# The masked relative bias of the neighbourhood heads: two products of rounded parts in place of one full-float product

## The chip, the core and the metric

The kernel runs on one core of a Trainium2 chip. The time is that of the device in microseconds (us), from the start to the end of one execution. It is measured over several runs; one further execution is recorded by the profiler, and its page and trace are read below.

## What is computed

Two layers of a diffusion backbone over 256 latent tokens (a grid of 4 rows of 64) with 256 context tokens. Each layer is feed-forward, token mixing, feed-forward. The mixing has three parts side by side: six neighbourhood heads of width 64, six heads of latent attention (MLA), and a state-space part. This case is about the neighbourhood heads' scores, in the reference:

```
s_win = einsum('brqhd,brkhd->bhrqk', qg, kg) * scale + bias      # bias: gathered from rpb by grid offset
s_win = where(in_win, s_win, NEG_INF)                            # 16 columns around the query
s_ctx = einsum('brqhd,bkhd->bhrqk', qg, kc) * scale
p = softmax(concatenate([s_win, s_ctx]))
```

Every latent query sees all 256 context keys and, of the 256 latent keys, those in its column window, with a learned bias that depends on the row and column distance. In layer 0 the context queries are computed too (over context keys, with no bias); in layer 1 only latent queries are.

## The kernel before

All activations lie transposed in SBUF. Almost all products are made by `mm3` (L287 to L293): each operand is split into a rounded part and the rest (type F32R), and three products of such parts stand for one full product. Full-float products are used in few places: transposes against the identity, scores, value products, and the product looked at here.

Weights come in units in a fixed order; `take` gives a unit, loads the one three ahead and splits the next (ScalarE copies to the rounded type, L251; VectorE or GpSimd subtracts, L252). Inside a unit the order of the work on every engine is the order in which the program writes it: each engine takes its own instructions in turn, and a waiting one holds up all that stand behind it on that engine.

`mixers` makes queries, keys and values, then calls `attention` (L1431), then multiplies by `w_out`. Just ahead of `attention` stand the last lines of the state-space gate: two copies on ScalarE (L1383) and one subtraction each on VectorE and GpSimd (both L1384). Before that, `bias` (128 x 36 x 64) has been filled by DMA with shifted rows of the bias table, its query columns running backwards; `window` (L1425, on GpSimd) adds the mask, 0 or -1e30, to six of its rows at a time, that is to one head. Heads 0 and 1 are masked before `attention`, head h + 2 while head h is scored.

`attention` opens its own pool of buffers and goes through a list of jobs: for each pair of heads, two query tiles per head ("x", latent queries), and in layer 0 one job per head for the context queries ("c"). Step i of its loop writes:

- `scores` of job i: for a neighbourhood head one product of queries and keys, 64 x 128 against 64 x 512 (L1458), then the bias product (L1463), which adds into the right half of the same sums: the constant matrix at `K_FLIP`, which turns the query columns back, times 256 columns of `bias`. Then the maximum on VectorE (L1470) and the Exp on ScalarE (L1474);
- `scale` of job i - 1: reciprocal and scaling on VectorE (L1479, L1481);
- `transposes` of job i - 3: four transposes on TensorE (L1490), emptied by VectorE or ScalarE in turn (L1493, L1495; L1498 for "c");
- at i = 4 `k_cols`: the transposes of the MLA keys (L1117, tile kn); at i = 6 the split of the next weights (`ahead`);
- `pv`, two steps after a pair is complete: value products (L1510), then a ScalarE copy and a VectorE subtraction that split the output (L1513, L1514).

Score sums have four buffers (`acc`), transposes three and sometimes a fourth.

Of the kernel before, what the change touches and what calls it, by code (L numbers as in the profile page):

```python
# [10 lines left out]
F32 = mybir.dt.float32  # L11
F32R = mybir.dt.float32r
AF = mybir.ActivationFunctionType
OP = mybir.AluOpType
# [22 lines left out]
K_ID, K_SEL, K_WIN, K_COS, K_SIN, K_DEL, K_ONE, K_FLIP, K_END = 0, 128, 130, 194, 258, 322, 338, 466, 594  # L37
# [56 lines left out]
class Net:  # L94
# [1336 lines left out]
    def attention(self, l, need, nq, nv, mq, mv, bias, ox, k_cols):  # L1431
        nc = self.nc
        V, P, S = nc.vector, nc.gpsimd, nc.scalar
        mm = nc.tensor.matmul
        with lines(self.tc, name=f"att{l}", bufs=1) as ap:
            def views(h):
                if h < 6:
                    r = slice(64 * (h % 2), 64 * (h % 2) + 64)
                    return nq[0][r, h // 2, :], nq[1][r, h // 2, :], lambda kt: nv[:, kt, 64 * h:64 * h + 64]
                return mq[0][:, h - 6, :], mq[1][:, h - 6, :], lambda kt: mv[:, kt, h - 6, :]  # L1440
# [8 lines left out]
                        jobs.append(("c", h, 0))  # L1449
            PT = {}  # L1450
            st = {}

            def scores(j):
                kind, h, t = j
                q, k, v = views(h)
                s = self.acc()
                if kind == "x":
                    mm(s, q[:, 256 + 128 * t:384 + 128 * t], k, start=True, stop=h >= 6)  # L1458
                    if h < 6:
                        if t == 0:  # L1460
                            self.window(bias, h + 2)
                        b = bias[:, 6 * h + 2 - 2 * t:6 * h + 6 - 2 * t, :].rearrange("p s k -> p (s k)")
                        mm(s[:, 256:512], self.k[:, K_FLIP:K_FLIP + 128], b, start=False, stop=True)  # L1463
                    nb, n = 1, 512
                else:
                    for i in range(2):
                        mm(s[:, 256 * i:256 * i + 256], q[:, 128 * i:128 * i + 128], k[:, 0:256], start=True, stop=True)
                    nb, n = 2, 256
                m = ap.tile([128, 2], F32, name="m", bufs=4)
                V.tensor_reduce(m[:, 0:nb], s.rearrange("p (b n) -> p b n", b=nb), axis=AX, op=OP.max, negate=True)  # L1470
                e = ap.tile([128, 512], F32, name="e", bufs=4)
                su = ap.tile([128, 2], F32, name="su", bufs=4)
                for i in range(nb):
                    S.activation(e[:, i * n:i * n + n], s[:, i * n:i * n + n], AF.Exp, bias=m[:, i:i + 1], accum_out=su[:, i:i + 1])  # L1474
                st[j] = (e, su, nb, n)
# [7 lines left out]
            def transposes(j):  # L1483
                kind, h, t = j
                e = st.pop(j)[0]
                if (kind, h) not in PT:
                    PT[kind, h] = ap.tile([128, 4 if kind == "x" else 2, 256], F32, name=f"PT{kind}", bufs=3)
                p = self.tp()
                for i in range(4):
                    nc.tensor.transpose(p[:, 128 * i:128 * i + 128], e[:, 128 * i:128 * i + 128], self.ident)  # L1490
                if kind == "x":
                    if t:
                        V.tensor_copy(PT[kind, h][:, :, 128 * t:128 * t + 128], p.rearrange("p (k q) -> p k q", k=4))  # L1493
                    else:
                        S.activation(PT[kind, h][:, :, 128 * t:128 * t + 128], p.rearrange("p (k q) -> p k q", k=4), AF.Copy)  # L1495
                    done = t == 1
                else:
                    S.activation(PT[kind, h].rearrange("p k (t q) -> p t k q", t=2), p.rearrange("p (t k q) -> p t k q", t=2, k=2), AF.Copy)  # L1498
                    done = True
                if done and h % 2:  # L1500
                    pend.append((kind, h))
# [17 lines left out]
            for i in range(len(jobs) + LAG):  # L1519
                if i < len(jobs):  # L1520
                    scores(jobs[i])
                if 0 < i <= len(jobs):
                    scale(jobs[i - 1])
                if i >= LAG:
                    transposes(jobs[i - LAG])
                if i == 4:
                    k_cols()
                if i == 6:
                    self.ahead()
                for a in old.pop(0):  # L1530
                    pv(*a)
                old.append(pend[:])
                pend.clear()
# [48 lines left out]
```

## Time and profile before

| | |
|---|---|
| time, median of 3 runs (lowest to highest) | 1960.9 us (1960.06 to 1961.4) |
| the profiled execution | 1962.65 us, of which the span from first to last instruction is 1960.7 us |
| TensorE (PE) busy | 1907.6 us, 97% of the span |
| VectorE (DVE), ScalarE (ACT), GpSimd (POOL) busy | 46%, 35%, 29% |
| mean granted clock of TensorE | 0.988 |

The clock is that which the chip granted to TensorE as a share of full speed, 2.4 GHz; the other level seen is 0.50, 1.2 GHz. Matmul records are pipelined: they overlap, and their ends are modelled, so the distance between the starts of neighbours is the better price. "PEld" is the loading of weights into the array, which can run beside a product. A full-float product leaves two records, a product of rounded parts one.

### The profile page before, as it was taken

What the parts mean: (1) busy time and instruction counts of PE and PEld (TensorE: products, weight loads), DVE (VectorE), ACT (ScalarE), POOL (GpSimd) and SP (SyncE); (2) the same over time, 40 slices, a digit from 0 to 9 for tenths busy, and PEclk for the clock granted to TensorE, in tenths of its full rate; (3) what the DMA queues carried; (4) which work ended last, traced back from release to release, by engine and by line L of the source; (5) the groups of instructions that cost most, each with busy time, mean ns of one, the idle gap of its engine ahead of it and who ended that gap; (6) DMA issues with size and microseconds to landing.
All of it is one profiled execution on the core that took longest, in us unless ns stands there. A gap on an engine that the chain in (4) does not pass through costs nothing.

```text
span 1960.7 us, 28001 instructions
## 1 busy us (share of the span) xinstructions
PE 1907.6 (97%) x11345; PEld 1557.8 (79%) x11345; DVE 907.3 (46%) x1596; ACT 678.8 (35%) x1128; POOL 574.3 (29%) x661
## 2 busy tenths in 40 slices
PE   7999999999999999999999999999999988999999
PEld 4777777788896587788888877777788878579999
DVE  6453233246457835232333554423433745655555
ACT  4421222224355634222212342122223435445343
POOL 2137461124535032100101314746212545231000
PEclk9999999999999999999999999999999999799999
DMA  9656566534431024533232455656523453036563
GB/s 309 178 166 200 174 205 212 165 97 141 132 105 51 2 86 130 173 117 96 88 105 76 139 158 167 201 160 217 178 75 113 141 166 100 22 126 215 175 194 108
DMA packets 364100, 277.75 MB, mean 142 GB/s; under 512 B 29854, under 2 KB 355812, under 8 KB 363972
## 3 DMA queue, kind: packets, MB, share of 16 engines
q1 hardware_dynamic: 361008, 268.44, 44.3%
q0 software_dynamic: 1888, 7.31, 1.0%
q8 instruction: 89, 1.46, 0.3%
q10 hardware_dynamic: 1076, 0.22, 0.1%
q14 instruction: 39, 0.32, 0.0%
HBM read 263.39 MB, written 12.55 MB: 141 GB/s over the span
## 4 chain that ended last, share of the span: by engine, by line
PE 84%; DVE 6%; POOL 4%; DMA 2%; ACT 1%; SPq 1%; issue 1%; POOLq 0%; ACTq 0%; DVEq 0%
PE acc L291 24%; PE acc L292 24%; PE acc L293 23%; PE b L467 3%; PE acc L1458 2%; PE t L1490 1%; DVE xm L562 1%; PE t L1510 1%; POOL ss L1134 1%; DVE xn L572 1%; PE acc L1463 1%; POOL sqs L523 1%; PE t L1100 1%; DMA bias<-in_na_rpb 1%; DVE xn L570 1%
## 5 line engine op out<-in xcount | busy, mean ns | idle before, releaser
L291 PE MATMUL acc<-xn,spl 128*128 128x512 f32 (+1 forms) x1664 | 598.0, 359 | 8.2 <-ACT mv L1340 5.9
L292 PE MATMUL acc<-xn,spl 128*128 128x512 f32 (+1 forms) x1664 | 590.7, 355 | 1.9 <-DVE xn L396 0.2
L293 PE MATMUL acc<-xn,spl 128*128 128x512 f32 (+1 forms) x1664 | 587.3, 353 | 0.1
L252 DVE TENSOR_TENSOR spl<-raw,spl 128x1024 fp32r<-128x1024 f32 (+2 forms) x312 | 390.2, 1287 | 276.0 <-ACT spl L251 273.8
L251 ACT ACTIVATE spl<-raw 128x1024 fp32r<-128x1024 f32 (+3 forms) x344 | 324.0, 990 | 303.9 <-PE acc L293 159.6
L291 PEld LDWEIGHTS acc<-xn,spl 128*128 128x128 f32 x1664 | 315.1, 189 | 71.7 <-issue 17.8
L292 PEld LDWEIGHTS acc<-xn,spl 128*128 128x128 f32 x1664 | 315.3, 189 | 46.7 <-DVE xn L570 4.3
L672 POOL TENSOR_TENSOR hid<-hv,hid 128x512 fp32r<-128x512 f32 (+1 forms) x88 | 101.8, 1156 | 852.2 <-ACT hid L671 852.2
L293 PEld LDWEIGHTS acc<-xn,spl 128*128 128x128 f32 x1664 | 315.3, 189 | 44.7 <-DVE spl L252 0.9
L291 PE MATMUL acc<-hid,spl 128*128 128x512 f32 (+1 forms) x740 | 265.2, 358 | 0.0
L292 PE MATMUL acc<-hid,spl 128*128 128x512 f32 (+1 forms) x740 | 262.0, 354 | 0.0
L293 PE MATMUL acc<-hid,spl 128*128 128x512 f32 (+1 forms) x740 | 261.7, 354 | 0.0
L669 DVE TENSOR_TENSOR hv<-sl,acc 128x512 f32<-128x512 f32 (+1 forms) x88 | 54.7, 621 | 365.1 <-PE acc L293 353.4
L671 ACT ACTIVATE hid<-hv 128x512 fp32r<-128x512 f32 (+1 forms) x88 | 50.9, 579 | 382.0 <-DVE hv L669 382.0
L729 DVE SCALAR_TENSOR_TENSOR h<-acc,mod,h 128x256 f32<-128x256 f32 x192 | 85.0, 479 | 210.8 <-PE acc L293 210.8
L291 PEld LDWEIGHTS acc<-hid,spl 128*128 128x128 f32 x740 | 139.8, 189 | 25.2 <-issue 6.4
L293 PEld LDWEIGHTS acc<-hid,spl 128*128 128x128 f32 x740 | 139.9, 189 | 19.7
L292 PEld LDWEIGHTS acc<-hid,spl 128*128 128x128 f32 x740 | 140.0, 189 | 18.5
L252 POOL TENSOR_TENSOR spl<-raw,spl 128x768 fp32r<-128x768 f32 (+3 forms) x32 | 65.3, 2041 | 211.4 <-ACT spl L251 199.5
L291 PE MATMUL acc<-spl,xn 128*128 128x384 f32 (+1 forms) x322 | 111.5, 346 | 0.0
L292 PE MATMUL acc<-spl,xn 128*128 128x384 f32 (+1 forms) x322 | 106.9, 332 | 0.4 <-POOL spl L252 0.3
L293 PE MATMUL acc<-spl,xn 128*128 128x384 f32 (+1 forms) x322 | 106.5, 331 | 0.0
(358 smaller groups left out, 1996.8 us busy)
## 6 DMA issues: line engine op xcount, KB each, us to landing
raw<-in_ffn_w_gu SPq DMA_DIRECT2D x176, 512.0 KB
raw<-in_w_mod SPq DMA_DIRECT2D x64, 1024.0 KB
raw<-in_ffn_w_down SPq DMA_DIRECT2D x32, 1024.0 KB
raw<-in_ffn_w_down SPq DMA_DIRECT2D x16, 768.0 KB
raw<-in_w_in SPq DMA_DIRECT2D x16, 768.0 KB
pmod<-in_w_mod SPq DMA_DIRECT2D x8, 1024.0 KB
raw<-in_w_out SPq DMA_DIRECT2D x8, 1024.0 KB
cld<-CL POOLq DMA_DIRECT2D x8, 576.0 KB, 4.8
```

Of the source, the lines that this page charges most:

```text
L251: nc.scalar.activation(s[:, 0, a:b], raw[:, a:b], AF.Copy)
L252: (nc.gpsimd if mix and b == n else nc.vector).tensor_tensor(s[:, 1, a:b], raw[:, a:b], s[:, 0, a:b].bitcast(F32), op=OP.subtract)
L291: mm(out, sl[0], sr[0], start=start, stop=False)
L292: mm(out, sl[0], sr[1], start=False, stop=False)
L293: mm(out, sl[1], sr[0], start=False, stop=stop)
L467: nc.tensor.matmul(p[32 * j:32 * j + 32, 0:256], self.cs[:, k, 6 - 2 * w:38 - 2 * w], raw[:, k, :], start=(a == 0 and w == 0), stop=(a == ...
L523: nc.gpsimd.tensor_tensor(self.sq_sum[:, c], self.sq_sum[:, c], s[:, c], op=OP.add)
L669: nc.vector.tensor_tensor(hv[:, c], sl[:, c], pu[:, c], op=OP.mult)
L671: nc.scalar.activation(hd[:, 0, c], hv[:, c], AF.Copy)
L672: nc.gpsimd.tensor_tensor(hd[:, 1, c], hv[:, c], hd[:, 0, c].bitcast(F32), op=OP.subtract)
L729: self.nc.vector.scalar_tensor_tensor(self.h[:, n, c], ps[:, c], self.mod[l][:, gate, n, s:s + 1], self.h[:, n, c], op0=OP.mult, op1=OP.add)
L1458: mm(s, q[:, 256 + 128 * t:384 + 128 * t], k, start=True, stop=h >= 6)
```

## The change

The full-float bias product is replaced by two products of rounded parts. At the start of `attention` VectorE copies the flip matrix into a tile of the rounded type. For each job of a neighbourhood head `parts` splits its 256 columns of the masked bias: ScalarE copies them to the rounded type, VectorE subtracts that from the original, which gives the second part. Both parts are multiplied by the flip matrix into the same sums. The parts of the first job are made ahead of the loop; those of each following job are written behind the bias products of the job before, ahead of that job's maximum. The parts have two buffers. The tiles for the transposed scores of the context jobs have two buffers instead of three.

```diff
             PT = {}
             st = {}
+            flip = ap.tile([128, 128], F32R, name="flip")
+            V.tensor_copy(flip, self.k[:, K_FLIP:K_FLIP + 128])
+            bp = {}
+
+            def parts(h, t):
+
+                if h < 6:
+                    b = bias[:, 6 * h + 2 - 2 * t:6 * h + 6 - 2 * t, :]
+                    bp[h, t] = ap.tile([128, 2, 4, 64], F32R, name="bp", bufs=2)
+                    S.activation(bp[h, t][:, 0], b, AF.Copy)
+                    V.tensor_tensor(bp[h, t][:, 1], b, bp[h, t][:, 0].bitcast(F32), op=OP.subtract)
+
+            parts(0, 0)
...
                     if h < 6:
                         if t == 0:
                             self.window(bias, h + 2)
-                        b = bias[:, 6 * h + 2 - 2 * t:6 * h + 6 - 2 * t, :].rearrange("p s k -> p (s k)")
-                        mm(s[:, 256:512], self.k[:, K_FLIP:K_FLIP + 128], b, start=False, stop=True)
+                        for i in range(2):
+                            mm(s[:, 256:512], flip, bp[h, t][:, i].rearrange("p s k -> p (s k)"), start=False, stop=i == 1)
+                        parts(*((h, 1) if t == 0 else (h + 1, 0)))
...
-                    PT[kind, h] = ap.tile([128, 4 if kind == "x" else 2, 256], F32, name=f"PT{kind}", bufs=3)
+                    PT[kind, h] = ap.tile([128, 4 if kind == "x" else 2, 256], F32, name=f"PT{kind}", bufs=3 if kind == "x" else 2)
```

## Rows read from the trace of the kernel before

**Rows 1.** The page: TensorE's busy time; the chain that ended last, by line.

```profile
PE 1907.6 (97%) x11345; PEld 1557.8 (79%) x11345; DVE 907.3 (46%) x1596; ACT 678.8 (35%) x1128; POOL 574.3 (29%) x661
...
PE acc L291 24%; PE acc L292 24%; PE acc L293 23%; PE b L467 3%; PE acc L1458 2%; PE t L1490 1%; DVE xm L562 1%; PE t L1510 1%; POOL ss L1134 1%; DVE xn L572 1%; PE acc L1463 1%; POOL sqs L523 1%; PE t L1100 1%; DMA bias<-in_na_rpb 1%; DVE xn L570 1%
```

**Rows 2.** By stretches: length, busy PE, PEld, DVE, ACT, POOL (instructions), clock, DMA share, GB/s.

```profile
630.00:640.00 10.00, 10.00 (x57) 5.79 (x56) 8.59 (x18) 5.60 (x16) 3.47 (x2) 1.00 0.33 106
```

**Rows 3.** Timeline, layer 0, mid-stage: start, duration, engine, line, tiles, shape, count.

```profile
626.22 0.70 PE L1463 MATMUL acc<-bias,k 128*128 128x256 f32 x2
626.75 0.60 PE L1490 MATMUL t<-k,e 128*128 128x128 f32 x4
...
628.33 0.70 PE L1463 MATMUL acc<-bias,k 128*128 128x256 f32 x2
...
631.52 1.95 PE L1510 MATMUL t<-PTx,nv 128*64 128x256 f32 x16
```

**Rows 4.** Timeline, layer 1, second feed-forward: products of rounded parts, 256 columns.

```profile
1749.82 0.28 PE L291 MATMUL acc<-xn,spl 128*128 128x256 f32 x1
1749.94 0.28 PE L292 MATMUL acc<-xn,spl 128*128 128x256 f32 x1
```

**Rows 5.** Timeline, layer 0, start of attention (in brackets: idle before, and releaser).

```profile
611.31 0.70 PE L1463 MATMUL acc<-bias,k 128*128 128x256 f32 x2
...
612.91 0.69 DVE L1384 TENSOR_TENSOR xn<-zq,xn 128x512 fp32r<-128x512 f32 x1
...
613.61 1.27 POOL L1384 TENSOR_TENSOR xn<-zq,xn 128x512 fp32r<-128x512 f32 x1 [3.50 <-ACT xn L1383]
...
614.91 1.29 DVE L1470 TENSOR_REDUCE m<-acc 128x1 f32<-128x512 f32 x2 [1.31 <-POOL xn L1384]
...
617.77 0.63 PE L1490 MATMUL t<-k,e 128*128 128x128 f32 x4 [0.72 <-DVE e L1481]
```

**Rows 6.** Timeline of TensorE at three waits; then stretches as in rows 2.

```profile
529.76 0.65 PE L1100 MATMUL t<-C,H 64*64 64x128 f32 x8 [1.30 <-POOL H L1083]
...
602.01 0.79 PE L291 MATMUL acc<-xn,spl 128*128 128x512 f32 x1 [3.41 <-ACT mv L1340]
...
1666.87 0.66 PE L1117 MATMUL t<-k,qn 128*96 128x128 f32 x2 [3.32 <-DVE mqT L1125]
...
606.00:608.00 2.00, 2.00 (x9) 1.54 (x8) 1.09 (x4) 1.78 (x3) 2.00 (x3) 0.55 0.00 0
...
1664.00:1686.60 22.60, 19.73 (x40) 8.92 (x41) 12.28 (x27) 8.25 (x20) 10.89 (x13) 0.55 0.00 1
1686.60:1700.00 13.40, 13.40 (x70) 7.54 (x67) 10.14 (x18) 7.96 (x16) 2.46 (x1) 1.00 0.02 7
```

**Rows 7.** Timeline, layer 1, start of attention, as in rows 5.

```profile
1669.89 1.22 PE L1463 MATMUL acc<-bias,k 128*128 128x256 f32 x2
...
1671.04 2.07 PE L1458 MATMUL acc<-nkT,nqT 64*128 64x512 f32 x2
...
1672.60 0.69 DVE L1470 TENSOR_REDUCE m<-acc 128x1 f32<-128x512 f32 x1 [0.77 <-POOL xn L1384]
...
1680.36 1.06 PE L1490 MATMUL t<-k,e 128*128 128x128 f32 x4
...
1685.22 1.06 PE L1117 MATMUL t<-k,kn 128*96 128x128 f32 x4
```

**Rows 8.** Timeline, layer 1, mid-stage: ScalarE and VectorE in one job.

```profile
1699.96 0.37 ACT L1513 ACTIVATE xn<-t 128x256 fp32r<-128x256 f32 x1
...
1700.37 0.42 DVE L1514 TENSOR_TENSOR xn<-t,xn 128x256 fp32r<-128x256 f32 x1
...
1700.71 0.68 DVE L1470 TENSOR_REDUCE m<-acc 128x1 f32<-128x512 f32 x1
...
1701.42 0.69 ACT L1474 ACTIVATE e<-acc,m 128x512 f32<-128x512 f32 x1 [1.09 <-DVE m L1470]
...
1702.10 0.59 ACT L1495 ACTIVATE PTx<-t 128x512 f32<-128x512 f32 x1
```

## Prediction

> **What bounds the kernel now.** I read the page first. TensorE is busy 97% of the span; the three lines of `mm3` hold 71% of the chain that ended last, the line of the bias product 1% [rows 1]. So a change to that product moves the time only by what it does to TensorE's order in `attention`, which runs once per layer. The table by stretches shows what kind of stage that is: in mid-stage TensorE has work in all of 10 us, VectorE in 8.6, ScalarE in 5.6, at the full clock [rows 2]. TensorE sets the end there, with VectorE close behind it. Next I read TensorE's own timeline in mid-stage, where the starts of neighbours give prices that the modelled ends don't. A bias product starts at 626.22, the transposes behind it at 626.75, the next job's bias product at 628.33: a job of a neighbourhood head takes 2.11 us, its bias product 0.53 [rows 3]. Last I read the start of the stage in either layer on all engines, since that is where the change puts new work ahead of the first bias product [rows 5, 7].
>
> **What is removed on TensorE.** 24 full-float bias products (6 heads, 2 query tiles, 2 layers; 48 records), each 0.53 us between starts [rows 3]. In their place come 48 products of rounded parts with the same 256 columns. The trace has that form elsewhere: in the second half of layer 1 `mm3` starts one every 0.12 us [rows 4]. I read the 0.53 as two records of about 0.213 plus 0.107 in which its first weight load stands open behind the 64-row score product, and keep the 0.107, since that neighbour stays. New price: 0.107 + 2 x 0.12 = 0.35 us, a gain of 0.187 us per job. If the second load stands open too the gain is 0.08, if none does 0.29. At half the clock the old product takes 1.15 us (1669.89 to 1671.04 [rows 7]): 0.30 and a stream of 0.85. The new pair's stream would double to about 0.43: 0.72 in all, a gain of 0.43. All 24 at full clock are worth 4.5 us, 0.23% of the time: no more is on offer there.
>
> **What is added off TensorE.** Per job a ScalarE copy of 128x256 and a VectorE subtraction of 128x256; the nearest rows of these shapes are 0.37 and 0.42 us [rows 8]. Once per layer a VectorE copy of 128x128 (I take 0.2 us, half of that subtraction, with 0.42 as the upper bound). Two buffers instead of three for the context heads' transposed scores cost nothing: their next use comes six jobs after, the product that frees them five jobs after. Summed, VectorE gets 10 us more and ScalarE 9 us more over both layers, under the cover of TensorE; but that cover is not loose. The copy for the next job stands in ScalarE's order behind the Exp of the job before, and the subtraction in VectorE's order ahead of the next maximum. This closes a circle that was not there: maximum to Exp 0.71, Exp to the next ScalarE instruction 0.68, copy to subtraction 0.41, subtraction to maximum 0.34 [rows 8], 2.14 us in all, and about 2.7 in every second job, where ScalarE also empties a transpose (0.59). Their mean of 2.42 meets TensorE's new pace, 2.11 - 0.187 plus a quarter of a value product of 1.95 us [rows 3], which is 2.41. In mid-stage it is a tie, and the transposes, which trail three jobs behind, give some 2.9 us of slack (two jobs of 2.11 less about 1.3 from maximum to scaled scores), so I let TensorE keep its gain there.
>
> **The wait at the start, layer 0.** Today the first bias product needs nothing from this stage and starts at 611.31 [rows 5]. VectorE, though, writes nothing in the stage's pool before 614.91: its first maximum waits there for GpSimd's subtraction of 613.61, and in layer 1 the first maximum (1672.60) is released by the same line [rows 5, 7]. In the new kernel the first writes into that pool are the flip copy and the first rounded part, and the bias product stands behind them: flip at 614.9, ScalarE copy 614.9 to 615.3, subtraction to 615.75, bias product at 615.8. If only VectorE's queue holds them back (its subtraction of 612.91 ends at 613.60), it is 614.35. So TensorE, in order, stands idle 3.0 to 4.5 us after its first score product, with all later scores and transposes behind it. I take 4.5. At full clock the first transposes would come at 621.1, because the maxima go at the circle's pace (616.35, 618.55, 620.75) and the fourth bias product needs the part subtracted just ahead of 620.75. That is 3.3 us after 617.77 [rows 5].
>
> **The clock.** Such a wait doesn't come alone. TensorE's wait of 3.41 us ahead of 602.01 and that of 3.32 us ahead of 1666.87 were each followed by work at half the clock, 1.2 GHz; one of 1.30 us (529.76) was not [rows 6]. 4.5 us is longer than either, so I expect the low clock from about 615 us. How long? Layer 1 goes through this stage's start at the low clock already: the mean from 1664 to 1686.6 is 0.55, though the engine works without a gap from 1667.9 on, and it is 1.00 only behind that [rows 6], once the transposes of the MLA keys have begun at 1685.22 [rows 7]. So I price layer 0 by layer 1's rows: from the first bias product to the first transposes 10.47 us (1669.89 to 1680.36), less 4 x 0.43 for the new form, 8.8. The transposes start at 615.8 + 8.8 = 624.6, 6.8 us late. Two sets of transposes (0.4 us more each) and one context score (1.05 more) at the low clock make it 8.7 late at the transposes of the MLA keys. I set their own low-clock stretch (+0.6) against TensorE's short waits for VectorE there now (-0.6). The remaining 8 jobs give back 8 x 0.187 = 1.5. Layer 0: +7.2 us.
> The Trainium skill (TensorE: Matmul & The Clock Gate, section "What's actually happening") says that the throttled state is the default and that activity releases it. Layer 1's rows, 17 us of recorded work at half the clock, agree only if these full-float products don't count as such activity; by the plain rule the low clock would end soon after the wait, which is the first rival below.
>
> **Layer 1.** The clock is low there before and after. The first bias product moves from 1669.89 to 1673.5 (the pool is free at 1672.6, then 0.4 for the copy and 0.45 for the subtraction): +3.6. Five jobs at the low clock give back 5 x 0.43 = 2.1, the transposes of the MLA keys slip behind the place where the clock rose (+0.6), and seven jobs at full clock give back 1.3. Layer 1: +0.8 us.
>
> **Sum.** The profiled execution took 1962.65 us (span 1960.7 and 1.95 around it), 1.75 above the median of the runs. 1962.65 + 7.2 + 0.8 = 1970.65; on the scale of the median 1968.9, so **1969 us**, 0.4% slower. A measurement of this kernel can tell about 0.2%, 3.9 us, from no change.
>
> **Rivals.**
> The clock returns with the work. After the wait ahead of 602.01 dense rounded products brought it back in 606 to 608 us (mean 0.55, so at 607.8 [rows 6]), 5.8 us after the wait. From 615.8 that is 621.6; the first transposes would start at 623.1, 5.3 us late. Less 1.5, plus layer 1's 0.8: 1965.5 us. Against it: layer 1's stretch.
> The clock doesn't fall. Then layer 0 is 3.3 less 1.5, with up to 1 us of VectorE's backlog on top: about +2.3, in sum 1964 us. Against it: both longer waits [rows 6].
> Not slower: the rounded pairs are dense work like that of 602 us, and lift the clock within the first two jobs of layer 1, so that two low-clock scores, two sets of transposes and one more score run at full rate. That takes some 4.7 us off layer 1 and 3 off layer 0's loss: 1961 us. It decides if the clock rises before about 1677. Against it: they are 0.43 us of a low-clock job of 3.7.
> Worse: the circle, not TensorE, sets the pace, and the low clock outlasts the transposes of the MLA keys in layer 0. No gain in mid-stage (+2.8), and four more jobs at 3.7 instead of 2.1 us (+6): 1977 us.
>
> **How the numbers follow.** Forecast 0.52 (its own range 1965 to 1973), clock returns 0.15, doesn't fall 0.13, lifted 0.08, worse 0.12. The range 1961 to 1977 reaches the ends of these. Faster by over 0.2% (below 1957) needs the full 4.5 us with no wait, or a clock lifted earlier still: 0.04. Within 0.2% (up to 1964.8): the lifted case, most of "doesn't fall" and a little of "returns", 0.22. Slower: 0.74.
>
> **What the new profile would show.** The wait: TensorE idle 3 to 4.5 us ahead of the first bias product of layer 0, released by VectorE's subtraction. The price: starts 0.35 us apart from bias pair to transposes in mid-stage. The clock: 0.50 from 615 to about 630 us. The circle: VectorE's subtraction waiting for ScalarE's copy in nearly every job. I am wrong in the main term if the clock stays at 1.00 there, and in the small ones if a job in mid-stage doesn't fall from 2.11 to about 1.93 us.

## The result and the profile after

The changed kernel takes 1984.0 us (median of 4 runs, 1979.8 to 1986.1), the kernel before beside it 1961.2 (4 runs, 1960.1 to 1962.3): a ratio of 1.0114, 95% interval 1.0096 to 1.0132. It is slower by 22.9 us. The forecast was 1969 with a range to 1977: the sign was right, the size was missed by 15 us, and the time lies outside the range.

The profiled execution of the changed kernel took 1979.84 us. Its page shows TensorE busy for nearly as long as before (1907.6 us, [rows 1]) in a longer span, and VectorE and ScalarE busier by 15.7 and 7.9 us:

```profile
PE 1910.4 (97%) x11345; PEld 1558.7 (79%) x11345; DVE 923.0 (47%) x1622; ACT 686.7 (35%) x1152; POOL 574.4 (29%) x661
```

All of the loss lies in the two runs of `attention`. Measured on TensorE from the first score product to the first product of the output projection, layer 0 went from 83.1 to 97.2 us and layer 1 from 65.3 to 72.5, together +21.2. Outside of it the two profiles differ only ahead of the first attention: that of before shows 6.8 us at the low clock from 539.5 us on and 6.8 from 601.0 on, that of after none and 3.4 us there, and its first attention starts 3.5 us earlier. So the two profiled executions differ by only 17.2 us. I cut each attention where the score products of the last job of a neighbourhood head start (in layer 0 that is the context job of head 5). The second halves, the MLA heads, are unchanged to 0.2 us. The whole 21 us is in the first halves: 42.6 to 56.6 us and 35.2 to 42.6 us.

**The start.** The timeline of after, layer 0; columns as in [rows 5], on whose place it stands:

```profile
606.76 1.12 PE L1471 MATMUL acc<-nkT,nqT 64*128 64x512 f32 x2
...
610.61 1.26 POOL L1384 TENSOR_TENSOR xn<-zq,xn 128x512 fp32r<-128x512 f32 x1 [2.47 <-ACT xn L1383]
...
611.90 0.87 DVE L1453 CAST flip<-k 128x128 fp32r<-128x128 f32 x1 [1.30 <-POOL xn L1384]
...
611.90 0.72 ACT L1461 ACTIVATE bp<-bias 128x256 fp32r<-128x256 f32 x2 [1.37 <-POOL xn L1384]
...
612.70 2.10 DVE L1462 TENSOR_TENSOR bp<-bias,bp 128x256 fp32r<-128x256 f32 x2
...
612.92 0.55 PE L1476 MATMUL acc<-bp,flip 128*128 128x256 f32 x1 [5.04 <-DVE flip L1453]
613.85 0.58 PE L1476 MATMUL acc<-bp,flip 128*128 128x256 f32 x1 [0.38 <-DVE bp L1462]
614.36 2.07 PE L1471 MATMUL acc<-nkT,nqT 64*128 64x512 f32 x2
...
622.41 1.05 PE L1504 MATMUL t<-k,e 128*128 128x128 f32 x4
```

Both first writes into the stage's pool (the flip copy, the first rounded part) start at 611.90, released by GpSimd's subtraction of L1384, as the prediction had it. TensorE waits 5.04 and 0.38 us, and then works at 1.2 GHz: a 64-row score product that took 1.12 us at 606.76 takes 2.07 at 614.36. By the trace's record the clock fell at 610.7, inside the wait, and came back at 627.7.

**The split.** The second place was not in the prediction. `ahead` issues the split of the next weights at job 6; on ScalarE and VectorE it stands between the parts of job 7 and those of job 8. This is what the timeline shows there in layer 0:

```profile
635.19 1.99 ACT L251 ACTIVATE spl<-raw 128x1024 fp32r<-128x1024 f32 x2
...
636.26 1.23 DVE L252 TENSOR_TENSOR spl<-raw,spl 128x1024 fp32r<-128x1024 f32 x1 [0.47 <-ACT spl L251]
637.08 0.40 ACT L1461 ACTIVATE bp<-bias 128x256 fp32r<-128x256 f32 x1
637.25 2.44 POOL L252 TENSOR_TENSOR spl<-raw,spl 128x1024 fp32r<-128x1024 f32 x1 [22.74 <-ACT spl L251]
637.51 2.46 DVE L1462 TENSOR_TENSOR bp<-bias,bp 128x256 fp32r<-128x256 f32 x1
637.53 0.38 PE L1476 MATMUL acc<-bp,flip 128*128 128x256 f32 x1 [1.21 <-ACT bp L1461]
...
640.02 0.58 PE L1476 MATMUL acc<-bp,flip 128*128 128x256 f32 x1 [2.11 <-DVE bp L1462]
```

The copy of the next part stands on ScalarE behind 1.99 us of the split; its subtraction stands on VectorE behind 1.23 us of it and then takes 2.46 us itself beside GpSimd's share. TensorE needs both parts at once and waits 1.21 and 2.11 us, and the clock falls again. Layer 1 repeats both places; TensorE's own timeline there (start, then the split):

```profile
1683.67 0.55 PE L1476 MATMUL acc<-bp,flip 128*128 128x256 f32 x1 [3.65 <-DVE flip L1453]
...
1709.26 0.38 PE L1476 MATMUL acc<-bp,flip 128*128 128x256 f32 x1 [1.13 <-ACT bp L1461]
...
1711.75 0.58 PE L1476 MATMUL acc<-bp,flip 128*128 128x256 f32 x1 [2.11 <-DVE bp L1462]
```

The table by stretches (columns as in [rows 2]; the mean granted clock stands behind the busy times) shows the low clock behind the start in layer 0, through the start in layer 1 (where before had it too [rows 6], for 20.5 us by the record instead of 23.9), and behind the split in layer 0:

```profile
612.92:629.60 16.68, 16.30 (x50) 9.52 (x50) 11.05 (x22) 7.88 (x19) 1.59 (x2) 0.56 0.01 1
1677.94:1702.00 24.06, 20.03 (x55) 10.42 (x54) 15.58 (x30) 10.81 (x25) 7.38 (x9) 0.55 0.00 1
637.50:645.00 7.50, 5.36 (x23) 3.02 (x23) 5.20 (x8) 2.84 (x7) 3.19 (x2) 0.54 0.43 140
```

Between the two places the products are what they were forecast to be. TensorE's timeline of after in mid-stage, to be held beside [rows 3]:

```profile
632.41 0.50 PE L1476 MATMUL acc<-bp,flip 128*128 128x256 f32 x2
632.75 0.60 PE L1504 MATMUL t<-k,e 128*128 128x128 f32 x4
...
634.33 0.51 PE L1476 MATMUL acc<-bp,flip 128*128 128x256 f32 x2
```

A pair takes 0.34 us from start to start where the full-float product took 0.53, and a job 1.92 us instead of 2.11.

### The profile page after: what moved, and what is told of

Its sections match the earlier page's. It is cut to its first block, busy times and chain, and to the rows that moved or that the text cites. A ratio compares the mean times of both kernels' runs of the same rounds, so it can differ in the third digit from the quotient of the medians.

```text
span 1977.9 us, 28057 instructions
## 1 busy us (share of the span) xinstructions
PE 1910.4 (97%) x11345; PEld 1558.7 (79%) x11345; DVE 923.0 (47%) x1622; ACT 686.7 (35%) x1152; POOL 574.4 (29%) x661
## 5 line engine op out<-in xcount | busy, mean ns | idle before, releaser
L252 POOL TENSOR_TENSOR spl<-raw,spl 128x768 fp32r<-128x768 f32 (+3 forms) x32 | 65.3, 2042 | 231.7 <-ACT spl L251 222.1
```

The source lines that it names most:

```text
L252: (nc.gpsimd if mix and b == n else nc.vector).tensor_tensor(s[:, 1, a:b], raw[:, a:b], s[:, 0, a:b].bitcast(F32), op=OP.subtract)
```

## The experiments

The theory after the comparison: the loss is two places per layer where TensorE waits, one at the start (pool not free) and one at the split (parts queued behind it), each with a stretch at the low clock. Rivals: GpSimd's slowing of VectorE makes the second one; the parts' own work sets the pace everywhere; the products are no gain at all. "First half" and "second half" are the pieces of `attention` defined above, from each run's profile, layer 0 / layer 1 in us:

| kernel | time, us | ratio to before, 95% | first halves | second halves |
|---|---|---|---|---|
| before | 1961.2 | | 42.6 / 35.2 | 40.6 / 30.1 |
| after | 1984.0 | 1.0096 to 1.0132 | 56.6 / 42.6 | 40.6 / 29.9 |
| e4 wait alone | 1974.7 | 1.0050 to 1.0080 | 52.7 / 38.7 | 40.6 / 30.1 |
| e2 split late | 1974.0 | 1.0051 to 1.0083 | 52.3 / 37.4 | 42.3 / 31.2 |
| e1 start early | 1975.2 | 1.0053 to 1.0091 | 53.8 / 39.7 | 40.6 / 29.9 |
| e3 both | 1966.4 | 1.0019 to 1.0039 | 46.5 / 33.7 | 42.3 / 31.2 |
| e6 no GpSimd | 1982.4 | 1.0090 to 1.0120 | 56.3 / 41.5 | 40.6 / 29.9 |
| e5 unread products | 1978.6 | 1.0066 to 1.0100 | 53.0 / 42.3 | 40.6 / 29.9 |
| e8 products alone | 1956.0 | 0.9961 to 0.9986 | 42.9 / 32.3 | 40.6 / 29.9 |
| e7 two jobs ahead | 1964.0 | 1.0003 to 1.0029 | 44.7 / 33.1 | 42.0 / 31.2 |
| e9 before, split late | 1965.0 | 1.0002 to 1.0022 | 43.1 / 35.7 | 42.0 / 31.4 |
| e10 e7, unread products | 1965.1 | 1.0004 to 1.0023 | 44.9 / 33.8 | 42.0 / 31.2 |
| e11 before, unread products | 1958.8 | 0.9978 to 0.9996 | 43.1 / 31.4 | 40.6 / 30.1 |
| e12 e7, split at job 6 | 1967.8 | 1.0026 to 1.0060 | 48.2 / 34.9 | 40.6 / 30.4 |
| e13 e7, split at job 12/8 | 1970.6 | 1.0040 to 1.0070 | 49.0 / 33.1 | 43.0 / 31.8 |

Runs of one chip share the runs of before (1962.5, 1961.6, 1962.1 and 1960.4 us in the four batches), so a difference to before is taken inside its batch; one between two versions of different batches carries 1 to 2 us of spread. Where a length of a low-clock stretch is given without a row, it is from the trace's record of the granted clock.

**The wait alone.** The kernel before, with its full-float product, but the flip matrix copied into the stage's pool first. Nothing else of the change is in it.

```
+            flip = ap.tile([128, 128], F32, name="flip")
+            V.tensor_copy(flip, self.k[:, K_FLIP:K_FLIP + 128])
...
-                        mm(s[:, 256:512], self.k[:, K_FLIP:K_FLIP + 128], b, start=False, stop=True)
+                        mm(s[:, 256:512], flip, b, start=False, stop=True)
```

> The kernel before, with one edit: VectorE copies the flip matrix into the stage's pool at its start, as full floats, and the unchanged full-float bias product reads that copy. No parts, no rounded products: only the wait of the first bias product for the pool is added. Theory (the wait and the low clock that it brings make the start's loss): the stage of layer 0 takes 5 to 9 us more than the 83.1 of the kernel before, with the clock at 0.50 from the wait on until the transposes of the MLA keys, that of layer 1 2 to 3 us more than 65.3: 1969 to 1974 us against 1962. Rival (the work on the parts makes the loss, not the wait): not above 1966 us, and no low clock in layer 0.

Measured: 1974.7 us, 13.1 over before. The timeline of VectorE and TensorE in layer 0:

```profile
614.36 0.87 DVE L1453 COPY flip<-k 128x128 f32<-128x128 f32 x1 [1.30 <-POOL xn L1384]
...
615.28 1.22 PE L1465 MATMUL acc<-bias,flip 128*128 128x256 f32 x2 [4.45 <-DVE flip L1453]
616.44 2.07 PE L1460 MATMUL acc<-nkT,nqT 64*128 64x512 f32 x2
```

A copy of 128x128 that nobody would notice by its own duration (0.87 us here, 0.22 in e1 below, ahead of the stage) costs 13 us, because it is the first write into a pool whose space GpSimd's subtraction still reads, and TensorE stands behind it. The first halves grow by 10.1 and 3.5 us, a little more than the 5 to 9 and 2 to 3 expected. The low clock lasts 17.1 us in layer 0, where there was none.

**The split moved behind the neighbourhood heads.**

```
-                if i == 6:
+                if i == (20 if need else 14):
                     self.ahead()
```

> The changed kernel with the split of the next weights moved from step 6 of the loop to behind the neighbourhood heads (step 20 in layer 0, 14 in layer 1). Theory: the second wait per layer (1.2 + 2.1 us of TensorE) and the 6.8 us of low clock behind it go, some 6.7 us per layer: 1970 to 1972 us against 1984; the subtraction of the parts takes 0.43 us in every job there instead of 2.46 in one. Rival (circle): the wait returns within the next jobs, and the time stays above 1978 us.

Measured: 1974.0 us, 10.0 under the changed kernel, though its second halves are 1.7 and 1.3 us longer; the 1970 to 1972 expected left that cost out. Waits of TensorE in layer 0's attention (engine, who waited for whom: us in total, times, longest), first of after, then of this kernel:

```profile
PE acc L1476 <- DVE flip L1453: 5.0, 1, 5.0
PE acc L1476 <- DVE bp L1462: 2.5, 2, 2.1
PE acc L1476 <- ACT bp L1461: 1.2, 1, 1.2
```

```profile
PE acc L1476 <- DVE flip L1453: 5.0, 1, 5.0
...
PE acc L1476 <- DVE bp L1462: 0.4, 1, 0.4
```

The wait for ScalarE's copy and that of 2.11 us for the subtraction are gone, and with them the second low-clock stretch; the wait at the start stays as it was.

**The start moved ahead.** The flip copy and the first two parts are made earlier, in columns of `xn` that are free then; later parts go to the pool as in the changed kernel.

```
+        flip = xn[:, 0, 2, 0:128]
+        V.tensor_copy(flip, self.k[:, K_FLIP:K_FLIP + 128])
...
+        parts(0, 0, None)
+        parts(0, 1, None)
         for j in range(6):
             self.transp(mq[0][:, j, 128 * qt_[0]:], lambda t: qs[t][:, j, :], 96, qt_, eng="act" if j % 2 else "dve")
```

> The changed kernel with its start alone undone: the flip copy and the parts of jobs (0,0) and (0,1) are made before the last transposes ahead of the stage, in columns of xn that are free then, so that no first write into the stage's pool stands before the first bias product. Theory (two waits per layer, each followed by the low clock): the start's share goes, about 8.5 us in layer 0 and 2 to 3 in layer 1, and the wait at the split of the next weights stays: 1972 to 1975 us against 1984 of the changed kernel. TensorE's clock stays at 1.00 at the start of layer 0. Rival (the circle of Exp, copy, subtraction and maximum sets the pace all through the neighbourhood heads): the start is worth no more than 3 us, 1980 us or more.

Measured: 1975.2 us, 8.8 under the changed kernel. Against the expectation the wait did not go; it moved two jobs on and halved. The first write into the pool is now the first maximum, and the copy for job (1, 0) stands on ScalarE behind the Exp that needs this maximum. This kernel's timeline:

```profile
612.86 0.69 DVE L1487 TENSOR_REDUCE m<-acc 128x1 f32<-128x512 f32 x1 [1.31 <-POOL xn L1399]
613.58 0.69 ACT L1491 ACTIVATE e<-acc,m 128x512 f32<-128x512 f32 x1 [0.80 <-DVE m L1487]
...
614.26 0.40 ACT L1386 ACTIVATE bp<-bias 128x256 fp32r<-128x256 f32 x1
...
614.76 0.55 PE L1479 MATMUL acc<-bp,xn 128*128 128x256 f32 x1 [2.47 <-POOL bias L1444]
615.62 0.58 PE L1479 MATMUL acc<-bp,xn 128*128 128x256 f32 x1 [0.30 <-DVE bp L1387]
```

The profile puts TensorE's wait down to GpSimd's work on `bias`; the copy of the part, which the product needs, ends at 614.66, just ahead of it. The low clock comes all the same (13.7 us in layer 0), and the split's waits and stretch are still there.

**Both.**

```
+        parts(0, 0, None)
+        parts(0, 1, None)
...
-                if i == 6:
+                if i == (20 if need else 14):
```

> Both edits: the start made early and the split moved late. Theory: both waits gone, the gain of 0.187 us on 24 products and 0.43 on those of layer 1's low clock is left: 1956 to 1961 us, 0 to 5 us below the kernel before. Rival (circle): 1964 us or more, with TensorE waiting for the parts in mid-stage.

Measured: 1966.4 us, 17.7 under the changed kernel, close to the sum of 10.0 and 8.8: the two losses are separate and add. But 3.9 us over before are left, and 1956 to 1961 was expected. The rival named the time, not the mechanism: in mid-stage TensorE waits 0.3 us at most for a part, but the moved wait of 2.47 us at the start of layer 0 is here too (0.50 more for the second part), with 10.2 us at the low clock.

**GpSimd kept out of the split.** VectorE does both of the split's subtractions while `attention` runs.

```
-            (nc.gpsimd if mix and b == n else nc.vector).tensor_tensor(s[:, 1, a:b], raw[:, a:b], s[:, 0, a:b].bitcast(F32), op=OP.subtract)
+            (nc.gpsimd if mix and b == n and not self.nopool else nc.vector).tensor_tensor(s[:, 1, a:b], raw[:, a:b], s[:, 0, a:b].bitcast(F32), op=OP.subtract)
...
                 if i == 6:
+                    self.nopool = True
                     self.ahead()
+                    self.nopool = False
```

> The changed kernel, but in the split of the next weights within attention VectorE makes both subtractions; GpSimd makes none there. Theory (the 2.46 us of one subtraction of parts come from GpSimd's subtraction of weights running at the same time): it takes 0.42 us, the second part's wait of TensorE shrinks from 2.11 to about 1 us, though VectorE has 1.23 us more: 1 to 3 us per layer, 1978 to 1982 us against 1984. Rival (it is the queue behind the split that costs, whoever subtracts): no change within 1 us, the subtraction of the parts stays above 1 us or its wait for TensorE the same length.

Measured: 1982.4 us, 1.7 under the changed kernel, with intervals that overlap. The timeline of this kernel at the split:

```profile
639.90 2.36 DVE L253 TENSOR_TENSOR spl<-raw,spl 128x1024 fp32r<-128x1024 f32 x2 [0.47 <-ACT spl L252]
...
641.17 0.39 PE L1477 MATMUL acc<-bp,flip 128*128 128x256 f32 x1 [1.20 <-ACT bp L1462]
642.17 0.42 DVE L1463 TENSOR_TENSOR bp<-bias,bp 128x256 fp32r<-128x256 f32 x1
642.64 0.39 PE L1477 MATMUL acc<-bp,flip 128*128 128x256 f32 x1 [1.09 <-DVE bp L1463]
```

Without GpSimd beside it the part's subtraction takes 0.42 us instead of 2.46: the slowing is real. But the time hardly moves, since VectorE now spends 2.36 us on the split itself, and ScalarE's copy is as late as before (wait of 1.20). What costs is the parts' place behind the split in two queues, not GpSimd's slowing by itself.

**Unread products in the start wait.** The changed kernel with 24 (layer 0) and 8 (layer 1) products of 128x512, whose result nobody reads, behind the first score product.

```
+                    if (h, t) == (0, 0):
+                        z = self.tp()
+                        for i in range(24 if need else 8):
+                            mm(z, ox[:, 0, 0, 0:128], ox[:, 0, 1, :], start=True, stop=True)
```

> The changed kernel with products that nobody reads put behind the first score product, 24 of 128x512 in layer 0 and 8 in layer 1, so that TensorE works while the first bias product waits (extra work, the result is unchanged). Theory (the clock is the larger part of the start's price): the clock stays at 1.00 through the wait of layer 0 and the stage there takes 91 to 94 us instead of 97.2. Rival (the waiting itself is the price, or the thin work behind it lets the clock fall anyway): 96 us or more, and 0.50 shortly after the filler ends.

Measured: 1978.6 us, 5.4 under the changed kernel though it does more. Its timeline at the start of layer 0:

```profile
610.78 5.76 PE L1475 MATMUL t<-xn 128*128 128x512 f32 x24
616.38 0.40 PE L1480 MATMUL acc<-bp,flip 128*128 128x256 f32 x2
...
621.94 0.60 PE L1508 MATMUL t<-k,e 128*128 128x128 f32 x4
```

The wait is filled and about as long (the first pair starts 6.65 us after the first score product, 6.16 in the changed kernel), and the clock stays at 2.4 GHz: the record of a pair is 0.40 us where it was 0.80. The stage of layer 0 takes 93.6 us, as expected. The transposes come 12.2 us after the first score product, against 15.7 in the changed kernel and 7.5 before (from 610.26 to 617.77, where [rows 5] have the transposes). Of the 8.1 us by which the changed kernel is late there, the wait makes 4.7 and the clock 3.4. In layer 1 the clock came back 4.6 us after the stage's start and fell again 3.4 us later, for 13.7 us.

**Products alone.** Parts of job (0, 0) only, made ahead of the stage; every pair uses them. The relative biases of all other jobs are left out, and with them the copies and subtractions per job; the split is at job 6 again.

```
-                            mm(s[:, 256:512], flip, bp[h, t][:, i].rearrange("p s k -> p (s k)"), start=False, stop=i == 1)
-                        parts(*((h, 1) if t == 0 else (h + 1, 0)))
+                            mm(s[:, 256:512], flip, bp[0, 0][:, i].rearrange("p s k -> p (s k)"), start=False, stop=i == 1)
```

> Only the rounded products, without work on parts: the parts of job (0,0) are made once per layer ahead of the last transposes, and every job's bias products read those, so the biases of the other jobs are left out. Split of the next weights at step 6 as before. Theory: 24 x 0.187 us and some 2 us more for layer 1's low clock: stage of layer 0 80.9 us, of layer 1 61.8, 1956 to 1958 us against 1962. Rival (the shorter products leave TensorE too little work at the start, and the clock falls in layer 0 without any wait for parts): layer 0 84 us or more, 1959 us or more.

Measured: 1956.0 us, 5.7 under before (2.7 to 7.7 by the interval). The prediction priced the products at 4.5. So the gain is there, and at the split TensorE has no wait that the kernel before lacks. But in the profiled execution (1958.6 us) it lies in layer 1 alone: 62.1 us against 65.3 there, 83.5 against 83.1 in layer 0, where 80.9 was expected. The rival's mechanism was seen in layer 0: the clock falls with no wait for parts, at 616.2 for 6.8 us, in this longer wait for the first scaled scores:

```profile
617.10 1.09 PE L1505 MATMUL t<-k,e 128*128 128x128 f32 x4 [1.52 <-DVE e L1496]
```

TensorE, faster through its first jobs, reaches the transposes 1.52 us before the first scaled scores are there; in the kernel before it was 0.72 [rows 5].

**Parts two jobs ahead.** Both corrections, and the parts in four places of `xn`, written two jobs before they are read, so that no part waits for the pool; three buffers again for the context heads. Against the changed kernel:

```
+                bp[h, t] = xn[:, t, 3 + h % 2].rearrange("p (i s k) -> p i s k", i=2, s=4)
...
-                        parts(*((h, 1) if t == 0 else (h + 1, 0)))
+                        parts(h + 1, t, None)
```

> As both edits together, and the parts are made two jobs ahead in four places of xn instead of one job ahead in two buffers, with three buffers for the context heads' tiles again. The copy of a job then no longer has to pass behind the Exp of the job just before its use, though the maximum still stands behind a subtraction that waits for a copy behind that Exp. Theory: the same as with both edits within 1 us, 1956 to 1961 us, since TensorE sets the pace in mid-stage. Rival (circle): the distance of two jobs takes waits of TensorE away, 3 us or more below the kernel with both edits.

Measured: 1964.0 us, 1.5 over before by the medians (0.6 to 5.7 by the interval) and 2.4 under the kernel with both edits; 1956 to 1961 was expected. The wait of 2.47 us is gone, and layer 0's first half is 1.8 us shorter for it. Its start has two short waits left:

```profile
613.02 0.38 PE L1477 MATMUL acc<-xn 128*128 128x256 f32 x1 [0.55 <-DVE xn L1385]
...
616.95 1.08 PE L1505 MATMUL t<-k,e 128*128 128x128 f32 x4 [0.70 <-DVE e L1496]
```

and still 10.2 us at the low clock, from 613.6 on, that is between the two. The first half of layer 1 is 2.2 us shorter than before, that of layer 0 2.1 longer.

**The late split in the kernel before.** The same edit as in e2, on the kernel before.

```
-                if i == 6:
+                if i == (20 if need else 14):
                     self.ahead()
```

> The kernel before with only the place of the split of the next weights moved to its later jobs (job 20 in the first layer, 14 in the second). It prices that move alone. Theory (the split costs the changed kernel its two waits of 1.2 and 2.1 us a layer and a low-clock stretch because the parts stand behind it in the queues of ScalarE and VectorE; the kernel before has no such parts there): nothing comes back here, attention 83 and 65 us as before, time within 3 us of before, 1959 to 1964. Rival (the split at job 6 costs any kernel, by what VectorE loses beside GpSimd): the attention shortens by 2 us or more a layer and the time is under 1957. Second rival (the late split delays the value-up of the MLA heads, which also need those engines): 1965 or more, and part of what the moved split left over in the kernel with both corrections is its own cost.

Measured: 1965.0 us, 2.9 over before. The expectation's second rival is what came: the first halves do not shorten, the second ones grow by 1.4 and 1.3 us. So the late place has a price of its own, no smaller than what e7 is behind the kernel before; e7's second halves are longer by 1.5 and 1.1 us, its first halves together the same.

**Unread products in the corrected kernel, and in the kernel before.** Eight of them behind the first score product of each layer: e7 with them (e10), the kernel before with them (e11).

```
+                    if (h, t) == (0, 0):
+                        z = self.tp()
+                        for i in range(8):
+                            mm(z, ox[:, 0, 0, 0:128], ox[:, 0, 1, :], start=True, stop=True)
```

> The kernel with both corrections and parts made two jobs ahead, with eight products of 128x512 whose result nobody reads put behind the first score product of each layer. Theory (what is left over before is the low clock at the attention's start, some 10 us in the first layer and 20 in the second): no low clock at the first layer's start, about 80 to 83 us there; in the second layer the clock comes back some 7 us in, about 58 to 61 us; the time 1955 to 1961, at or under the kernel before. Rival (what is left over is work of the parts on ScalarE and VectorE, by the circle): the clock rises and the time still stays at 1962 to 1966, with waits of TensorE for the parts or the row maximum in every job.

> The kernel before with the same eight unread products of 128x512 behind the first score product of each layer: the control for the one above. Theory: the first layer, at full clock there anyway, pays at most the 1.9 us of the products, partly inside the waits at the start; the second layer gets its clock back earlier than 20 us and gains 3 to 5 us; the time 1956 to 1961. If this control gains as much as the kernel above, then the fillers do not make the rounded products better than the full-float one, they only show what the low clock costs either.

Measured: 1965.1 us, no gain over e7, where 1955 to 1961 was expected; 1958.8 us in the kernel before, a gain of 3.3 as expected. In the kernel before the low clock of layer 1 lasts 6.8 us instead of 20.5, and its first half 31.4 instead of 35.2. In the corrected kernel layer 0 fell to the low clock later (621.9 us, for 6.8 us, behind a wait of 0.91 for scaled scores), and layer 1 had it for 13.7 us and again for 3.4, from 1690.2 on, in a wait of 1.92 for VectorE to empty transposes. So the fillers there cost 2.0 us in layer 0 (613.14 to 615.10) and 3.6 in layer 1 (1675.05 to 1678.63) and gave back no more. The rival was not seen either: TensorE did not wait for parts in every job. Why the same products hold the clock in one order of work and not in the other stays open.

**The split back among the neighbourhood heads, with parts two jobs ahead.** e7 with the split at job 6 (e12), or at job 12 and 8 (e13).

```
-                if i == (20 if need else 14):
+                if i == 6:
                     self.ahead()
```

```
-                if i == (20 if need else 14):
+                if i == (12 if need else 8):
                     self.ahead()
```

> The kernel with parts made two jobs ahead, with the split of the next weights back at job 6. Theory (the late place of the split costs 1.3 to 1.5 us in the second half of each layer's attention, 2.4 us of the time in the kernel before, and parts made two jobs, some 3.9 us, ahead cover a split of 2 to 3.3 us): no wait of TensorE for a part at the split, no low clock there, second halves of 40.6 and 30 us again, and the time 2 us under that of the late split, 1960 to 1963, equal to the kernel before. Rival (two jobs are not enough, since the split delays both the copy on ScalarE and the subtraction on VectorE): waits of 1 us or more at job 8, a low-clock stretch behind them, the first half 3 to 5 us longer, 1966 to 1970.

> The same with the split at job 12 in the first layer and 8 in the second, later among the neighbourhood heads, where the stretch at low clock at the start is over and the parts have their full lead. Theory: as with job 6, no wait at the split, second halves of 40.6 and 30 us, 1960 to 1963. Rival one (two jobs are not enough): the wait of 1 us or more and the low clock sit at job 14, 1966 to 1970. Rival two (the split costs the same 1.5 us wherever it stands, by what VectorE loses beside GpSimd): no wait for a part, yet the first half longer by 1.5 us, 1963 to 1966.

Measured: 1967.8 and 1970.6 us, 3.8 and 6.6 over e7's median (each with its own runs of before, 7.4 and 10.2 over them). In e12 the second halves are back at 40.6 and 30.4 us and TensorE waits 0.5 us at most for a part, as the theory had it, but the first halves grow by 3.5 and 1.8, so its time failed. The rival named the time, not the mechanism, since the long wait for a part is absent. In e13 the first halves grow by 4.3 and 0.0 us over e7, and the second ones, which were to shrink, by 0.9 and 0.6. All engines' timeline of e12 at the split:

```profile
634.07 2.45 POOL L252 TENSOR_TENSOR spl<-raw,spl 128x1024 fp32r<-128x1024 f32 x1 [17.60 <-ACT spl L251]
634.33 2.47 DVE L1385 TENSOR_TENSOR xn<-bias,xn 128x256 fp32r<-128x256 f32 x1
...
636.72 0.68 DVE L1485 TENSOR_REDUCE m<-acc 128x1 f32<-128x512 f32 x1
...
638.14 0.63 PE L1505 MATMUL t<-k,e 128*128 128x128 f32 x4 [0.77 <-DVE e L1496]
```

A part two jobs ahead still stands in VectorE's queue ahead of the next maximum: the subtraction of 2.47 us holds that up to 636.72, and TensorE waits for scaled scores instead of parts. In e13 layer 0 also fell to the low clock at 653.8 for 10.2 us, behind waits of no more than 0.9 us.

None of the complete versions of the new product beats the kernel before; e7 comes nearest.

## Why the prediction was wrong, and where it was right

Step by step, as stretches of TensorE's timeline in the profiled executions, after less before:

| step | forecast | measured |
|---|---|---|
| price of a pair in mid-stage | 0.35 us, job 1.93 | 0.34, job 1.92 |
| pair at the low clock | 0.72 | 0.73 (616.36 to 617.09) |
| first bias product, after the first score, layer 0 | 5.5 us | 6.2 |
| first transposes there | +6.8 | +8.1 |
| transposes of the MLA keys, layer 0 | +8.7 | +9.9 |
| score product of job 8, layer 0 | +8.3 | +9.3 |
| first bias product, layer 1 | +3.6 | +3.7 |
| score product of job 8, layer 1 | +1.5 | +2.1 |
| from there to the end, layer 0 | -1.1 | +4.7 |
| from there to the end, layer 1 | -0.7 | +5.1 |
| sum | +8.0 | +21.2 |

(The forecasts at job 8 take its own terms: 8.7 less two pairs of 0.187, and 3.6 - 2.1 + 0.6 less three.) Job 8 is the one whose parts stand behind the split. Up to it the forecast holds to 1.0 and 0.6 us. At the split it loses 5.8 us in each layer, 11.6 of the 13.2 missed in the profile.

**The step that failed** is the sentence that the copies and subtractions lie "under the cover of TensorE; but that cover is not loose". The prediction then tested the cover in one job only, by the circle from maximum to maximum [rows 8], in a stretch where the split of the next weights does not stand. The split stands in the same two queues in the middle of the stage: the list of the loop's steps names it, and the profile of before has it. These rows, at the place where the table by stretches was read [rows 2], were never priced:

```profile
628.36 1.99 ACT L251 ACTIVATE spl<-raw 128x1024 fp32r<-128x1024 f32 x2
...
629.43 1.22 DVE L252 TENSOR_TENSOR spl<-raw,spl 128x1024 fp32r<-128x1024 f32 x1 [0.47 <-ACT spl L251]
630.42 2.46 POOL L252 TENSOR_TENSOR spl<-raw,spl 128x1024 fp32r<-128x1024 f32 x1 [13.08 <-ACT spl L251]
...
631.36 1.81 DVE L1481 TENSOR_SCALAR e<-e,su 128x512 f32<-128x512 f32 x1
```

Before, the delay of the row maximum and of the scaled scores was absorbed: the transposes trail three jobs behind, and the bias product needed neither engine. After, the bias product of the very next job needs both. An estimate from these rows alone: a copy that starts 2 us late, and a subtraction that ends no sooner than the scaling beside GpSimd's 2.46 us did (633.17), would have held TensorE some 3 us at the bias product of job 8, which started at 630.45; 3.3 was measured. By the prediction's own reading of [rows 6], where the waits of 3.3 and 3.4 us came with the low clock, a second low stretch was to be reckoned with. That was a rival to write down; with the 5.8 us per layer that it came to, the sum is 1980. The rivals listed all turned on the clock behind the start or on the circle.

**What was right.** The wait at the start, its place, its releaser and its length (5.0 and 0.4 us against 3.0 to 4.5, over the upper bound by 0.9), and the low clock with it (17.1 us, where some 15 were forecast). e4 prices this step alone at 13.1 us of the time. The prediction's own numbers make it 8.7 + 4 x 0.43 = 10.4 in layer 0 and 3.6 in layer 1, 14.0. The 1.3 us by which the first transposes were later than forecast come from two terms. The pool was free 5.1 us after the first score product (611.90 less 606.76) instead of 4.65. And VectorE stood beside GpSimd's work on `bias`, 2.69 us from 611.83 on: the flip copy took 0.87 us (forecast 0.2, bound 0.42; it takes 0.22 ahead of the stage in e1), the two subtractions 1.05 each (forecast 0.42). The price of a pair is right at either clock, and e8 measures a gain of 5.7 us, with 4.5 in its interval. But in e8's profile layer 0 shows none of its share of 2.2 us, and 6.8 us at the low clock with no wait for a part, which the sum did not have. Every kernel with the rounded products but the one with 24 fillers (e5) fell to the low clock in the first jobs of layer 0; the kernels with the full-float product and no added wait (before, e9, e11) did not.

The Trainium skill (TensorE: Matmul & The Clock Gate, section "What's actually happening") has it that activity releases the throttle. For this stage's work, most of it full-float products and transposes, the trace of after does not bear that out: TensorE has work in 16.3 of 16.7 us from 612.92 on and the mean clock is 0.56. For dense products of rounded parts it does: in e11, with eight of them, the low clock of layer 1 lasted 6.8 us instead of 20.5, and with the fillers of e5 the start of layer 0 stayed at full clock. So the rival "the clock returns with the work" failed, as forecast.

**The circle** was called a tie, and in mid-stage it cost nothing: VectorE's subtraction does wait for ScalarE's copy in most jobs, yet TensorE kept its 1.92 us a job. It decided where something lengthened one of its steps, as the split does in e12.

**What stays open.** Of the 22.9 us, the wait with its clock is 13.1 (e4), the split 10.0 (e2) and 2.9 more for the late place that this run paid (e9); less the products' 4.5 that makes 21.5. The 1.4 us left are no more than the spread between batches, so a price of the parts' own work isn't shown. Whether the two buffers instead of three for the context heads cost anything was not tried by itself; no profile shows a wait for them. And what makes the clock fall in e7 behind a wait of 0.55 us, when it did not in the kernel before behind one of 0.72 [rows 5], is not settled.

## What to carry to other kernels

Work that moves from one long product on the bounding engine to preparation on two side engines isn't priced by its duration but by what else stands in those engines' queues at every place of the stage: walk through the whole stage, not one clean job, and price each burst there (here a split of 2 to 2.5 us, 5.8 us a layer). The first write into a pool inherits the release time of whatever used that space, so a copy of less than 1 us on the path of the bounding engine can cost 13 us; make such constants earlier, elsewhere, and look which write is then the first (in e1 the wait passed on to it). And a correction that moves a burst away has a price where the burst lands (2.9 us here): measure it in the kernel before as well.

## What the runs showed of the hardware

VectorE beside GpSimd: a subtraction of 128x256 with two inputs takes 0.42 us alone (e6) and 2.46 when GpSimd's subtraction of 128x1024 (2.44 us) starts just ahead of it; it ends 0.28 us behind GpSimd's. A scaling with one tensor input took 1.81 instead of 0.49 in the kernel before, while a maximum over scores in PSUM takes 0.68 in either case (630.58 in before, beside the same GpSimd row). The Trainium skill (GPSIMD Engine Reference, section "Specifications") says that GpSimd's interfaces to SBUF are shared with VectorE, for instructions of VectorE in a 2-port mode or with two SBUF inputs. For the subtraction, which has two, the trace agrees and gives the size, in effect the whole of GpSimd's instruction; in which mode the scaling ran no run shows. Not every instruction of GpSimd does this: beside its product of 128x6 (1.32 us at 605.63 in e1) two subtractions of 128x256 took 0.38 us each.

The clock does not follow the length of a wait: TensorE waited 1.52 us in e8 and had 6.8 us at 1.2 GHz, but 0.55 in e7 and had 10.2. With the longer waits of 3.3 to 5.0 us at the start of a stage (before in layer 1; after, e2 and e4 in both) the stretch among these full-float products lasted 17 to 24 us.
